# Second half of the out-product and the MLP's first steps from one table of times with the attention

## The chip, the cores and the metric

The kernel runs on one core of a Trainium2 chip, in one launch. The metric is the time on the device in microseconds. Before the change it is 1292.5 us in the median of three runs (1292.22 to 1293.47). The engines are named as in the profile: PE (TensorE), DVE (VectorE), ACT (ScalarE), POOL (GpSimd), SP (SyncE, which here only issues DMAs).

## What is computed

One layer of an encoder on 1024 tokens of 1024 features, in float32:

```
h  = rms(x) * norm1_g
p  = h @ w_in
a  = mlstm_group(conv + silu of p's q and k, v, o, gates)     # 4 heads of 128, both directions
b  = diff_attention_group(q, k, v of p, relative bias)        # 4 heads, softmax - lam * softmax
x  = x + concat(a, b) @ w_out
u  = (rms(x) * norm2_g) @ w_ff1
x  = x + relu(u)**2 @ w_ff2
```

## The kernel before

**Products.** A float32 product is made on PE in three passes of the shorter type fp32r (`mm3`): each operand is cut into a high half (a copy on ACT, `hi`) and a low half (the difference, on DVE or POOL, `lo`); the passes are hi·hi, hi·lo and lo·hi, so that the third matmul of a tile is the first to need the low half of the weights. A matmul has 512 columns here, the transposes and `pav` 128.

**Stages.** From 0 to about 370 us of the span: the projections of x and the mLSTM in small pieces. From 374 to 605: the attention, 32 items (half of the sequence, head, block of 128 queries), with the first half of the out-product (tokens 0 to 511) in between. Then the second half of the out-product (tokens 512 to 1023), and from 660.8 the MLP, up to the end.

**Order.** Inside an engine, instructions run in the order in which the program issues them, and a waiting instruction holds all behind it. Two ways set the order. In the attention a table `A` of times (in items) and `when(t, f, ...)` put small pieces on a heap, and they are issued by ascending time. The mLSTM uses the same heap with its own times, and the MLP a list of its own. The other way is code written out by hand: the second half of the out-product is the generator `out_product(1, psum1)`, whose steps alternate with `row_norms`, `normed`, `cut` and `load_e`, the entry of the MLP:

```
    for n, _ in enumerate(work):
        if n == 2:
            next(norms, None)
        if 3 <= n < 7:
            j = n - 3
            normed(0, j)
            cut(*x_part(1 + j // 2, block(j // 2, 0), j % 2))
        if 6 <= n < 10:
            with tc.issue_after(rooted[0]):
                cut(w_a(n - 6), raw_e[n - 6])
            if n < 8:
                load_e(n - 4)
```

**The out-product's second half.** It has eight tiles n of 128 features; each takes 24 matmuls of 512 columns (8 blocks k in the order 4, 5, 6, 0, 1, 2, 3, 7, three passes each) into the bank `pw1n`. Its weights come as `raw_wo1n` (512 KB, two buffers), `hi_wo1n` and `lo_wo1n` (three buffers each). DVE adds x into `y1` (the row is called `y`), ACT squares it, and DVE sums the squares in `yacc`. `row_norms` makes the row sums on PE (`pr`), adds EPS on DVE, takes the power -0.5 on POOL (`rc`) and spreads the result over the partitions on PE (`pb`). `normed` multiplies y by it, and `cut` makes the halves of the MLP's operands: x1, x2 and later x3 to x7 from y, `wa0`, `wa1`, `wb`, `we` from the loads `re0` to `re3` of w_ff1.

**The attention.** For an item, `pl` are the logits, `l` the weights, `pa` their transposes on PE, `at` DVE's copy of them, `pav` the product with v, `sm` the factors of the rows, `on` the normalised result (DVE). After four items of a head `pt` turns them on PE, and ACT and DVE write the halves into `mix`. In the mLSTM, `pzTrue` are transposes of the stabiliser's rows and `zzTrue` their scaled copies; `pad`, the taps of q and k and `qs` are DVE's, `lo_va` is POOL's low half of the weights of the attention's v.

**In the MLP** `m` are the products, `sq` differences of them, `ro` the odd loads of w_ff1, `z` the products with w_ff2.

Of the kernel before, what the change touches and what calls it, by code (L numbers as in the profile page):

```python
# [10 lines left out]
F32 = mybir.dt.float32  # L11
# [5 lines left out]
P = 128  # L17
# [31 lines left out]
def hybrid_block_kernel(ctx: ExitStack, tc: tile.TileContext, xT, w_v, w_kg, w_c, w_va, w_qa, w_o, w_1, w_2, vec, rel, onehot, outT):  # L49
# [38 lines left out]
    def rsqrt(out, x, n):  # L88
        return nc.gpsimd.tensor_tensor(out, x, mhalf[:, 0:n], op=ALU.pow)
# [67 lines left out]
    def mm3(out, ahi, alo, bhi, blo, start, stop):  # L157
        nc.tensor.matmul(out, ahi, bhi, start=start, stop=False)  # L158
        nc.tensor.matmul(out, ahi, blo, start=False, stop=False)  # L159
        latest[0] = nc.tensor.matmul(out, alo, bhi, start=False, stop=stop).ins  # L160
# [114 lines left out]
            step()  # L275


    clock, table, made = [0.0], [], []

    def when(t, f, *args):  # L280
        heapq.heappush(table, (t, len(made), f, args))
        made.append(t)

    def tick():
# [742 lines left out]
    r2, acc, rooted = {}, {}, {}

    def out_product(half, psum):
        sl = slice(half * HB, (half + 1) * HB)  # L1030
        acc[half] = opool.tile([P, HB], F32, tag="yacc", name=f"yacc{half}")
        order = (4, 5, 6, 0, 1, 2, 3, 7)
        ps, ws = {}, {}

        def load(n):
            if n < KT:
                ws[n] = split(opool, w_o[n], "wo", opool, 3, 2, nc.vector, f"wo{half}{n}")

        def part(n, first, end):
            if first == 0:  # L1040
                load(n)
                ps[n] = psum(n)
            (whi, wlo), p = ws[n], ps[n]
            for j in range(first, end):
                k = order[j]
                kt = slice(k * P, (k + 1) * P)
                mm3(p, whi[:, kt], wlo[:, kt], mix[half][k][:, 0], mix[half][k][:, 1], j == 0, j == KT - 1)


        part(0, 0, KT - 1)  # L1050
        part(1, 0, KT // 2)
        yield
        part(1, KT // 2, KT - 1)
        for n in range(KT):
            if n < 2:
                part(n, KT - 1, KT)
            else:
                part(n, 0, KT // 2)
                yield
                part(n, KT // 2, KT)  # L1060
            p = ps[n]
            yt = y[half][n]
            nc.sync.dma_start(yt, xT[n][:, sl])
            nc.vector.tensor_tensor(yt, p, yt, op=ALU.add)
            if n == 0:
                nc.scalar.activation(acc[half], yt, AF.Square)
            else:
                sq = opool.tile([P, HB], F32, tag="ysq", name=f"ysq{half}{n}", bufs=1)
                nc.scalar.activation(sq, yt, AF.Square)
                nc.vector.tensor_tensor(acc[half], acc[half], sq, op=ALU.add)  # L1070
            nc.scalar.dma_start(y_dram[half][n], yt)
            yield

    def row_norms(half):
        pc = psF.tile([P, HB], F32, tag="q2", name=f"pr2{half}")
        for t in range(4):
            nc.tensor.matmul(pc[:, t : t + 1], acc[half][:, t * P : (t + 1) * P], ones[:, 0:1], start=True, stop=True)
        rc = mpool2.tile([P, 4], F32, tag="rc", name=f"rc2{half}")
        nc.vector.tensor_scalar(rc, pc[:, 0:4], D * EPS, None, op0=ALU.add)
        rooted[half] = rsqrt(rc, rc, 4).ins  # L1080
        yield
        p = psF.tile([P, HB], F32, tag="q3", name=f"pb2{half}")
        for t in range(4):
            nc.tensor.matmul(p[:, t * P : (t + 1) * P], rc[:, t : t + 1].to_broadcast([P, P]), ident, start=True, stop=True)
        r2[half] = mpool2.tile([P, HB], F32, tag=("v", "w")[half], name=f"r2{half}")
        nc.vector.tensor_copy(r2[half], p)
# [93 lines left out]
    def w_out(n):  # L1180
        raw = opool.tile([P, 1024], F32, tag="raw", name=f"raw_wo0{n}", bufs=2)
        hi = opool.tile([P, 1024], F32R, tag="woh", name=f"hi_wo0{n}", bufs=3)
        return hi, opool.tile([P, 1024], F32R, tag="wol", name=f"lo_wo0{n}", bufs=3), raw
# [40 lines left out]
    def item_pieces(n, it):  # L1224
        def on(name, f, *args):
            when(n + A[name], f, it, *args)

        if n % 4 == 0:
            when(n + A["LD"] if n else -98.0, att_load, it)
            when(n + A["LV"] if n else -97.0, att_load_v, it)  # L1230
        for m in range(2):
            on(f"G{m}", att_logits, m)
            on(f"E{m}", att_exp, m)
            on(f"A{m}", att_across, m)
            on(f"C{m}", att_copy, m)
# [16 lines left out]
    last = {}
    while table:
        t, _, f, args = heapq.heappop(table)
        f(*args)
    order.close()
    load_mix(1)
# [6 lines left out]
    work = out_product(1, psum1)
    next(work)
    att_turn(items[28:32], last)
    att_hi(items[31], last)
    att_lo(items[31], last)
# [73 lines left out]
    next(norms)
    for n, _ in enumerate(work):
        if n == 2:
            next(norms, None)
        if 3 <= n < 7:
            j = n - 3
            normed(0, j)
            cut(*x_part(1 + j // 2, block(j // 2, 0), j % 2))
        if 6 <= n < 10:  # L1350
            with tc.issue_after(rooted[0]):
                cut(w_a(n - 6), raw_e[n - 6])
            if n < 8:
                load_e(n - 4)
# [510 lines left out]
```

## Time and profile before

| | us |
|---|---|
| median of three runs | 1292.5 |
| the profiled execution | 1292.14 |
| its span | 1290.4 |
| PE busy | 1257.0 |
| DVE busy | 860.0 |
| ACT busy | 603.5 |
| POOL busy | 272.6 |

The span reaches from the first to the last instruction of the profiled execution, and 1.7 us of its time lie around it. Rows give times from the span's start. An engine's busy time is the sum over its instructions; where PE is nearly always busy, the reader looks for the few stretches in which it stands still and for what ended each of them.

### The profile page before, as it was taken

The numbers are of one execution on the slowest core, as the hardware profiler recorded it, in microseconds if no ns is written. First come the engines' busy times: TensorE is split into PE (matmuls) and PEld (weight loads), VectorE is DVE, ScalarE is ACT, GpSimd is POOL, SyncE is SP. The second block draws the span as 40 slices with busy tenths as digits, with TensorE's granted clock in tenths as the row PEclk, the third lists the DMA queues.
The fourth block names the chain that finished last, engine by engine and source line by source line (L and its number), as shares of the span: only waits on it lengthen the run. The fifth ranks groups of instructions, "written<-read, shape, count | busy, mean of one in ns | idle before, by whom it ended". The sixth has DMA issues, their size and how long they took to land.

```text
span 1290.4 us, 17143 instructions
## 1 busy us (share of the span) xinstructions
PE 1257.0 (97%) x6443; PEld 1038.3 (80%) x6443; DVE 860.0 (67%) x1159; ACT 603.5 (47%) x1033; POOL 272.6 (21%) x273
## 2 busy tenths in 40 slices
PE   8999999999999989999999999999999999999998
PEld 6898678887878877888777788888887888888887
DVE  8635547886338888786748887666664675458754
ACT  5323336676535565563526554454444343333332
POOL 6623312554234344332000000000000000004001
PEclk9999999999999999999989999999999999999999
DMA  6415054544165475526524574454439946344732
GB/s 201 135 54 175 24 190 108 123 123 147 72 201 195 146 263 189 177 98 214 179 95 158 188 244 163 148 163 131 154 118 330 328 163 212 116 145 148 236 114 90
DMA packets 101459, 208.32 MB, mean 161 GB/s; under 512 B 8688, under 2 KB 21744, under 8 KB 101376
## 3 DMA queue, kind: packets, MB, share of 16 engines
q1 hardware_dynamic: 78368, 154.50, 37.6%
q10 hardware_dynamic: 15008, 31.50, 6.5%
q0 software_dynamic: 8000, 21.24, 5.0%
q8 instruction: 50, 0.82, 0.3%
q14 instruction: 33, 0.27, 0.1%
HBM read 148.90 MB, written 58.29 MB: 161 GB/s over the span
## 4 chain that ended last, share of the span: by engine, by line
PE 83%; DVE 8%; DMA 3%; issue 2%; ACT 2%; POOL 1%; SPq 0%; DVEq 0%; ACTq 0%; POOLq 0%
PE z L1707 8%; PE z L1705 8%; PE z L1706 8%; PE m L1376 7%; PE m L1377 7%; PE m L1378 7%; PE pav L986 4%; PE pl L945 3%; PE pv L235 3%; PE pw L158 2%; PE pa L972 2%; PE pw L160 2%; PE pw L159 2%; PE pj_c L158 2%; PE pj_c L159 2%
## 5 line engine op out<-in xcount | busy, mean ns | idle before, releaser
L1743 POOL TENSOR_TENSOR zx<-zx,res 128x512 f32<-128x512 f32 x4 | 8.7, 2180 | 503.8 <-DVE zx L1741 503.8
L1707 PE MATMUL z<-wbh,wa0l 128*128 128x512 f32 x224 | 87.4, 390 | 0.6 <-DVE wa0l L1296 0.6
L1705 PE MATMUL z<-wbh,wa0h 128*128 128x512 f32 x224 | 87.2, 389 | 0.0
L1706 PE MATMUL z<-wbl,wa0h 128*128 128x512 f32 x224 | 87.2, 389 | 0.0
L1706 PE MATMUL z<-wel,wa1h 128*128 128x512 f32 x224 | 87.1, 389 | 0.0
L1705 PE MATMUL z<-weh,wa1h 128*128 128x512 f32 x224 | 87.1, 389 | 0.0
L1707 PE MATMUL z<-weh,wa1l 128*128 128x512 f32 x224 | 87.1, 389 | 0.0
L950 DVE CUSTOM_DVE_ANT_0 l<-pl,toe 128x1024 f32<-128x1024 f32 x64 | 76.3, 1221 | 15.5 <-PE pl L945 14.4
L956 ACT ACTIVATE l<-l,sm 128x1024 f32<-128x1024 f32 x64 | 72.9, 1141 | 1.3 <-DVE sm L950 1.3
L1296 DVE TENSOR_TENSOR wel<-g,weh 128x1024 fp32r<-128x1024 f32 x28 | 35.2, 1258 | 56.5 <-ACT weh L1293 56.5
L1425 ACT ACTIVATE sq<-sq 128x512 f32<-128x512 f32 x48 | 30.3, 632 | 90.6 <-DVE sq L1464 69.0
L1296 DVE TENSOR_TENSOR wbl<-g,wbh 128x1024 fp32r<-128x1024 f32 x28 | 35.4, 1265 | 55.9 <-ACT wbh L1293 55.9
L1293 ACT ACTIVATE weh<-g 128x1024 fp32r<-128x1024 f32 x28 | 29.7, 1060 | 90.2 <-PE z L1707 53.4
L1293 ACT ACTIVATE wbh<-g 128x1024 fp32r<-128x1024 f32 x28 | 29.7, 1061 | 89.9 <-PE z L1707 52.6
L986 PEld LDWEIGHTS pav<-v,at 128*128 128x128 f32 x512 | 62.9, 195 | 9.3 <-DVE on L1001 4.6
L986 PE MATMUL pav<-v,at 128*128 128x128 f32 x512 | 64.4, 280 | 4.5 <-DVE on L1001 2.9
L160 PE MATMUL pw<-mix,lo_wo 128*128 128x512 f32 x128 | 51.5, 402 | 4.2 <-DVE lo_wo L134 4.2
L158 PE MATMUL pj_c<-hhi,hi_c 128*128 128x512 f32 x128 | 53.5, 418 | 0.0
L945 PE MATMUL pl<-kk,q 64*128 64x512 f32 x384 | 53.3, 408 | 0.0
L158 PE MATMUL pw<-mix,hi_wo 128*128 128x512 f32 x128 | 53.2, 415 | 0.0
L159 PE MATMUL pw<-mix,hi_wo 128*128 128x512 f32 x128 | 51.1, 399 | 0.0
L159 PE MATMUL pj_c<-hlo,hi_c 128*128 128x512 f32 x128 | 50.7, 396 | 0.0
(459 smaller groups left out, 3680.2 us busy)
## 6 DMA issues: line engine op xcount, KB each, us to landing
g<-g_dram SPq DMA_DIRECT2D x56, 512.0 KB, 4.1
g_dram<-gs SPq DMA_DIRECT2D x64, 256.0 KB, 4.3
g_dram<-sq ACTq DMA_DIRECT2D x42, 256.0 KB, 2.2
kk<-k_dram POOLq DMA_DIRECT2D x16, 512.0 KB, 5.6
raw_wo<-in_w_o_dram SPq DMA_DIRECT2D x16, 512.0 KB, 4.7
re<-in_w_dram SPq DMA_DIRECT2D x16, 512.0 KB, 4.4
ro<-in_w_dram SPq DMA_DIRECT2D x16, 512.0 KB, 3.7
zt<-in_w_dram SPq DMA_DIRECT2D x16, 512.0 KB, 4.1
```

What stands on the lines that cost most here:

```text
L158: nc.tensor.matmul(out, ahi, bhi, start=start, stop=False)
L159: nc.tensor.matmul(out, ahi, blo, start=False, stop=False)
L160: latest[0] = nc.tensor.matmul(out, alo, bhi, start=False, stop=stop).ins
L945: nc.tensor.matmul(it.pl[x][:, sl], hd.q[r, i, qi * P : (qi + 1) * P], hd.kk[r, j, sl], start=n == 0, stop=n == 2)
L950: nc.vector.tensor_tensor_reduce(lt, it.pl[m], hd.toe[:, off : off + S], 1.0, 3.0e38, ALU.add, ALU.min, it.sm[:, m : m + 1])
L986: nc.tensor.matmul(it.pav[:, 0:P], at, it.head.v[:, c], start=c == 0, stop=c == NC - 1)
L1376: nc.tensor.matmul(p, wh, xh, start=go, stop=False, skip_group_check=True)
L1377: nc.tensor.matmul(p, wh, xl, start=False, stop=False, skip_group_check=True)
L1378: nc.tensor.matmul(p, wl, xh, start=False, stop=stop and k == 3, skip_group_check=True)
L1705: nc.tensor.matmul(p, wh, gh, start=go, stop=False, skip_group_check=True)
L1706: nc.tensor.matmul(p, wh, gl, start=False, stop=False, skip_group_check=True)
L1707: nc.tensor.matmul(p, wl, gh, start=False, stop=end, skip_group_check=True)
```

## The change

The generator `out_product` goes. Its steps become pieces of the table `A`, so that the second half of the out-product and the MLP's first steps are sorted in with the last items of the attention, on every engine: loads with their space (`h_room`, `split_ahead` with a floor in time), matmuls (`h_part`), the sum with x (`h_add`), squares (`h_square`), their sum (`h_sum`), the two steps of `row_norms`, `normed`, and the cuts of x1, x2 and of the first four tiles of w_ff1, high half and low half apart. Besides, 42 pieces of the heap of the attention and the mLSTM and 24 of the MLP's list get an offset to their own time (`moved`), and one entry of `A`, the low half of `mix`, is 0.026 later.

```diff
+    moved = {
+        20: 0.16, 25: -2.784, 36: 2.075, 37: 0.745, 43: -0.133, 92: 2.944, 95: 2.082, 122: -0.259, 124: 2.027,
...
     def when(t, f, *args):
-        heapq.heappush(table, (t, len(made), f, args))
+        heapq.heappush(table, (t + moved.get(len(made), 0.0), len(made), f, args))
...
-        OA=1.385, OW=-3.888, OH=-2.551, OL=-2.267,
+        OA=1.385, OW=-3.888, OH=-2.551, OL=-2.267, HF=34.3, HS=0.375, LM=33, HE=0.3, HQ=0.415, HA=0.425, HW=-1.4,
+        HH=-0.861, HL=-0.4, HX=-3.083, S2=35.3, N0=36.2, N1=36.9, XN=37.278, XD=0.78, XH=1.108, XL=1.118, WN=37.523,
...
-        floor = A["SW"] + 0.01 if pre == "O" else -99.0
+        floor = max(floor, A["SW"] + 0.01 if pre in "OH" else -99.0)
...
-        if n % 4 == 3 and n < 31:
+        if n % 4 == 3:
...
+    def h_part(V, n, first, end):
+        if first == 0:
+            V[0] = psum1(n)
+        k_order = (4, 5, 6, 0, 1, 2, 3, 7)
+        hi, lo, _ = V["w"][0]
+        for j in range(first, end):
+            k = k_order[j]
+            kt = slice(k * P, (k + 1) * P)
+            mm3(V[0], hi[:, kt], lo[:, kt], mix[1][k][:, 0], mix[1][k][:, 1], j == 0, j == KT - 1)
+
+    def h_room(n):
+        nc.sync.dma_start(y[1][n], xT[n][:, HB:])
+
+    def h_add(V, n):
+        nc.vector.tensor_tensor(y[1][n], V[0], y[1][n], op=ALU.add)
...
+    def h_sum(V, n):
+        if n > 0:
+            nc.vector.tensor_tensor(acc[1], acc[1], V["sq"], op=ALU.add)
...
+    parts_at = {0: ((0, 0, 7), (3.5, 7, 8)), 1: ((1.75, 0, 4), (2.75, 4, 7), (3.75, 7, 8))}
+    ends = {0: 3.75, 1: 4.0}
+    for n in range(2, KT):
+        parts_at[n] = ((2 * n, 0, 4), (2 * n + 1, 4, 8))
+        ends[n] = 2 * n + 2.0
+    def room_at(n):
+        return A["HF"] + u * ends[n - 3] + 0.01 if n > 2 else -99.0
+
+    for n in range(KT):
+        t = A["HF"] + u * parts_at[n][0][0]
+        V = {"w": split_ahead(lambda n=n: w_out(n, 1), w_o[n], nc.vector, t, "H", room_at(n))}
+        for p, first, end in parts_at[n]:
+            when(A["HF"] + u * p, h_part, V, n, first, end)
+        t = A["HF"] + u * ends[n]
+        when(max(t + A["HX"], A["S2"] + 0.02), h_room, n)
+        when(t + A["HE"], h_add, V, n)
+        when(t + A["HQ"], h_square, V, n)
+        when(t + A["HA"], h_sum, V, n)
...
+    when(A["N0"], next, norms)
+    when(A["N1"], next, norms, None)
+    for j in range(4):
+        t = A["XN"] + j * A["XD"]
+        when(t, normed, 0, j)
+        when(t + A["XH"], lambda a: cut_hi(*a), x_part(1 + j // 2, block(j // 2, 0), j % 2))
+        when(t + A["XL"], lambda a: cut_lo(*a), x_part(1 + j // 2, block(j // 2, 0), j % 2))
+        t = A["WN"] + j * A["WD"]
+        when(A["RE"] if j < 2 else t - 2 * A["WD"] + A["WL"] + 0.01, load_e, j)
+        when(t, lambda c: cut_hi(w_a(c), raw_e[c]), j)
+        when(t + A["WL"], lambda c: cut_lo(w_a(c), raw_e[c]), j)
...
     def when(t, f, *args):
-        table.append((t, len(table), f, args))
+        table.append((t + moved.get(len(table), 0.0), len(table), f, args))
```

DVE, in the out-product's second half, before: `y0` and `x2` belong to the MLP's entry, `lo_wo16` and `lo_wo17` are the low halves of the weights of tiles 6 and 7.

```order
L1064 TENSOR_TENSOR y1_1_5787<-pw13_5897,y1_1_5787 128x512
L1296 TENSOR_TENSOR x1l_5791<-y0_1_4383,x1h_5790 128x1024
L1070 TENSOR_TENSOR yacc1_5721<-yacc1_5721,ysq13_5928 128x512
L1328 SCALAR_TENSOR_TENSOR y0_2_4384<-y0_2_4384,cst_185,r20_5889 128x512 x2
L1328 SCALAR_TENSOR_TENSOR y0_3_4385<-y0_3_4385,cst_185,r20_5889 128x512 x2
L1296 TENSOR_TENSOR x2l_5793<-y0_2_4384,x2h_5792 128x1024
L1064 TENSOR_TENSOR y1_2_5788<-pw14_5942,y1_2_5788 128x512
L1296 TENSOR_TENSOR x2l_5793<-y0_3_4385,x2h_5792 128x1024
L1070 TENSOR_TENSOR yacc1_5721<-yacc1_5721,ysq14_5973 128x512
L134 TENSOR_TENSOR lo_wo16_6030<-raw_wo16_6028,hi_wo16_6029 128x1024
L134 TENSOR_TENSOR lo_wo17_6069<-raw_wo17_6067,hi_wo17_6068 128x1024
L1064 TENSOR_TENSOR y1_2_5788<-pw15_5991,y1_2_5788 128x512
```

DVE at the same place after the change.

```order
L1233 TENSOR_TENSOR y1_1_5790<-pw13_5893,y1_1_5790 128x512
L1077 TENSOR_TENSOR lo_wo15_5908<-raw_wo15_5906,hi_wo15_5907 128x1024
L1244 TENSOR_TENSOR yacc1_5863<-yacc1_5863,ysq13_5971 128x512
L1305 TENSOR_TENSOR wa0l_5798<-re0_5828,wa0h_5797 128x1024
L1337 SCALAR_TENSOR_TENSOR y0_1_4383<-y0_1_4383,cst_185,r20_5917 128x512 x2
L1337 SCALAR_TENSOR_TENSOR y0_2_4384<-y0_2_4384,cst_185,r20_5917 128x512 x2
L1233 TENSOR_TENSOR y1_2_5791<-pw14_5939,y1_2_5791 128x512
L1305 TENSOR_TENSOR x1l_5794<-y0_0_4382,x1h_5793 128x1024
L1077 TENSOR_TENSOR lo_wo16_5954<-raw_wo16_5952,hi_wo16_5953 128x1024
L1244 TENSOR_TENSOR yacc1_5863<-yacc1_5863,ysq14_6017 128x512
L1305 TENSOR_TENSOR wa1l_5800<-re1_5830,wa1h_5799 128x1024
L1233 TENSOR_TENSOR y1_2_5791<-pw15_5979,y1_2_5791 128x512
```

`lo_wo16` now stands ahead of the sum with the fourth tile's squares and of both cuts of x2, and `lo_wo15` behind tile 3; cuts of w_ff1 (`wa0l`, `wa1l`), which stood further ahead, come between.

SP's queue of DMA issues at the start of the second half, before: `raw_wo1n` are the out-product's weights, `re` w_ff1, `y1` the pieces of x.

```order
L131 DMA raw_wo12_5847<-in_w_o_dram 128x1024
L131 DMA raw_wo13_5891<-in_w_o_dram 128x1024
L131 DMA raw_wo14_5936<-in_w_o_dram 128x1024
L1312 DMA re0_5806<-in_w_1_dram 128x1024
L1312 DMA re1_5808<-in_w_1_dram 128x1024
L1063 DMA y1_0_5786<-in_xT_dram 128x512 x2
L1063 DMA y1_1_5787<-in_xT_dram 128x512 x2
L1063 DMA y1_2_5788<-in_xT_dram 128x512
L131 DMA raw_wo15_5985<-in_w_o_dram 128x1024
```

The same queue after the change.

```order
L1070 DMA raw_wo12_5737<-in_w_o_dram 128x1024
L1230 DMA y1_0_5789<-in_xT_dram 128x512 x2
L1230 DMA y1_1_5790<-in_xT_dram 128x512 x2
L1230 DMA y1_2_5791<-in_xT_dram 128x512
L1321 DMA re0_5828<-in_w_1_dram 128x1024
L1321 DMA re1_5830<-in_w_1_dram 128x1024
L1070 DMA raw_wo13_5838<-in_w_o_dram 128x1024
L1230 DMA y1_2_5791<-in_xT_dram 128x512
L1070 DMA raw_wo14_5857<-in_w_o_dram 128x1024
```

The loads of tiles 3 and 4 went behind five loads of x and two of w_ff1.

DVE in the mLSTM, about 190 us into the span, before: `q0` are taps of the convolution of q, `k4` of k, `pad` is the padded row that they read.

```order
L342 SCALAR_TENSOR_TENSOR zzTrue12_1742<-pzTrue12_1737,cst_185,zzTrue12_1742 128x512
L650 SCALAR_TENSOR_TENSOR q0_1689<-pad_1677,vecs_183,q0_1689 128x1024
L342 SCALAR_TENSOR_TENSOR zzTrue13_1764<-pzTrue13_1759,cst_185,zzTrue13_1764 128x512
L650 SCALAR_TENSOR_TENSOR q0_1689<-pad_1677,vecs_183,q0_1689 128x1024
L646 TENSOR_TENSOR pad_1677<-pj_c4_1682,rb_212 128x1024
L650 SCALAR_TENSOR_TENSOR k4_1788<-pad_1677,vecs_183,k4_1788 128x1024 x4
```

DVE at the same place after the change.

```order
L350 SCALAR_TENSOR_TENSOR zzTrue12_1742<-pzTrue12_1737,cst_185,zzTrue12_1742 128x512
L658 SCALAR_TENSOR_TENSOR q0_1695<-pad_1677,vecs_183,q0_1695 128x1024 x2
L350 SCALAR_TENSOR_TENSOR zzTrue13_1777<-pzTrue13_1772,cst_185,zzTrue13_1777 128x512
L654 TENSOR_TENSOR pad_1677<-pj_c4_1682,rb_212 128x1024
L658 SCALAR_TENSOR_TENSOR k4_1788<-pad_1677,vecs_183,k4_1788 128x1024 x4
```

The piece of `zzTrue13` goes behind the last tap of q and directly ahead of `pad` of the next row; on PE its transposes `pzTrue13` go 12 matmuls back.

## Rows read from the trace of the kernel before

**Rows 1.** The page: busy time of each engine, and the chain that ended last

```profile
PE 1257.0 (97%) x6443; PEld 1038.3 (80%) x6443; DVE 860.0 (67%) x1159; ACT 603.5 (47%) x1033; POOL 272.6 (21%) x273
PE 83%; DVE 8%; DMA 3%; issue 2%; ACT 2%; POOL 1%; SPq 0%; DVEq 0%; ACTq 0%; POOLq 0%
```

**Rows 2.** PE's waits: line waited for, us in total, times, longest us

```profile
PE pw L160 <- DVE lo_wo L134: 4.2, 1, 4.2
...
PE pva L159 <- POOL lo_va L603: 2.6, 2, 1.6
PE m L1376 <- DVE sq L1464: 2.4, 1, 2.4
...
PE m L1377 <- DVE x7l L1296: 0.8, 2, 0.5
```

**Rows 3.** PE in time: start, us, line, op, out<-in, count [idle before <-releaser]

```profile
625.49 1.16 PE L1084 MATMUL pb<-ident,rc 128*128 128x128 f32 x8 [1.43 <-POOL rc L89]
...
643.06 0.39 PE L159 MATMUL pw<-mix,hi_wo 128*128 128x512 f32 x1
647.63 0.80 PE L160 MATMUL pw<-mix,lo_wo 128*128 128x512 f32 x1 [4.18 <-DVE lo_wo L134]
...
652.49 0.63 PE L159 MATMUL pw<-mix,hi_wo 128*128 128x512 f32 x1
```

**Rows 4.** Stretches: us, busy by engine (count), granted PE clock, DMA share, GB/s

```profile
420.00:480.00 60.00, 55.80 (x386) 46.95 (x388) 50.18 (x89) 33.42 (x72) 23.72 (x45) 0.97 0.61 195
600.00:610.00 10.00, 9.99 (x65) 8.66 (x64) 4.26 (x7) 2.92 (x7) 2.06 (x7) 1.00 0.82 289
640.00:650.00 10.00, 5.82 (x22) 4.42 (x21) 9.31 (x12) 4.18 (x5) 0.00 (x0) 0.82 0.09 32
650.00:660.00 10.00, 10.00 (x39) 8.14 (x38) 2.08 (x3) 0.66 (x2) 0.00 (x0) 0.84 0.14 52
```

**Rows 5.** ACT and DVE in time, ahead of the late low half

```profile
637.79 1.04 ACT L133 ACTIVATE hi_wo<-raw_wo 128x1024 fp32r<-128x1024 f32 x1
...
640.17 2.73 DVE L1328 SCALAR_TENSOR_TENSOR y<-y,cst,r 128x512 f32<-128x512 f32 x4
...
646.35 2.36 DVE L134 TENSOR_TENSOR lo_wo<-raw_wo,hi_wo 128x1024 fp32r<-128x1024 f32 x2
```

**Rows 6.** The tile `raw_wo`, 560 to 660 us: its loads

```profile
DMA to landing us min/median/max: 3.5/3.9/6.0
```

**Rows 7.** DVE and PE in time, end of the attention

```profile
578.52 3.17 DVE L134 TENSOR_TENSOR lo_wo<-raw_wo,hi_wo 128x1024 fp32r<-128x1024 f32 x1
...
587.20 0.66 PE L1008 MATMUL pt<-ident,on 128*128 128x128 f32 x4 [0.64 <-DVE on L1001]
```

**Rows 8.** PE and DVE in time, first products of the MLP

```profile
699.10 0.50 PE L1378 MATMUL m<-x5h,wel 128*128 128x512 f32 x1 [0.35 <-DVE wel L1296]
...
710.23 0.68 DVE L1464 TENSOR_TENSOR sq<-w,m 128x512 f32<-128x512 f32 x1
```

**Rows 9.** DVE in time, ahead of the first `z`

```profile
980.39 1.22 DVE L1296 TENSOR_TENSOR wa0l<-za,wa0h 128x1024 fp32r<-128x1024 f32 x1
```

**Rows 10.** ACT, DVE and PE in time, mLSTM

```profile
190.10 0.69 ACT L148 ACTIVATE zzTrue<-pzTrue,cst 128x512 fp32r<-128x512 f32 x1 [1.19 <-PE pzTrue L334]
...
192.87 1.23 DVE L646 TENSOR_TENSOR pad<-pj_c,rb 128x1024 f32<-128x1024 f32 x1
...
204.28 0.66 PE L705 MATMUL pk<-ident,k 128*128 128x128 f32 x4 [0.41 <-ACT k L148]
```

**Rows 11.** DVE, POOL and ACT in time, halves of the attention's v weights

```profile
292.99 1.76 DVE L756 TENSOR_TENSOR qs<-q,qs 128x1024 f32<-128x1024 f32 x1
...
293.62 3.35 POOL L603 TENSOR_TENSOR lo_va<-raw_va,hi_va 128x1024 fp32r<-128x1024 f32 x1
...
297.06 1.04 ACT L148 ACTIVATE hi_va<-raw_va 128x1024 fp32r<-128x1024 f32 x1
```

**Rows 12.** DVE in time, an item of the attention

```profile
467.65 0.35 DVE L1001 TENSOR_SCALAR on<-pav,sm 128x128 f32<-128x128 f32 x1 [0.48 <-POOL sm L89]
```

More of the change, by code (lines that the diff above doesn't have):

```diff
@@ L275, in drain @@
             step()
+    moved = {
[5 rows of a table added]
+    }
     clock, table, made = [0.0], [], []
     def when(t, f, *args):
-        heapq.heappush(table, (t, len(made), f, args))
+        heapq.heappush(table, (t + moved.get(len(made), 0.0), len(made), f, args))
         made.append(t)
@@ L1025, in load_mix @@
             nc.gpsimd.dma_start(mix[half][h], mx_dram[h][half])
[L1027 to L1072, printed above, removed]
+    r2, acc = {}, {}
     def row_norms(half):
@@ L1079, in row_norms @@
         nc.vector.tensor_scalar(rc, pc[:, 0:4], D * EPS, None, op0=ALU.add)
-        rooted[half] = rsqrt(rc, rc, 4).ins
+        rsqrt(rc, rc, 4)
         yield
@@ L1092, in hybrid_block_kernel, with split_ahead @@
         G0=-0.05, G1=0.219, E0=0.984, E1=1.396, W=1.626, A0=2.667, A1=2.819, C0=2.714, C1=2.824, P=3.534, SQ=3.666,
-        RS=3.676, ON=3.783, TU=4.131, TH=4.141, TL=4.151, LD=-2.901, LV=-1.095, PF=-4, PS=1.015, PE=0.388, PT=1.671,
+        RS=3.676, ON=3.783, TU=4.131, TH=4.141, TL=4.177, LD=-2.901, LV=-1.095, PF=-4, PS=1.015, PE=0.388, PT=1.671,
         PB=1.957, PW=-3.566, PH=-2.613, PL=-1.973, PX=-0.258, SW=15.195, OF=18.423, OS=0.979, OE=0.323, OQ=0.587,
-        OA=1.385, OW=-3.888, OH=-2.551, OL=-2.267,
+        OA=1.385, OW=-3.888, OH=-2.551, OL=-2.267, HF=34.3, HS=0.375, LM=33, HE=0.3, HQ=0.415, HA=0.425, HW=-1.4,
+        HH=-0.861, HL=-0.4, HX=-3.083, S2=35.3, N0=36.2, N1=36.9, XN=37.278, XD=0.78, XH=1.108, XL=1.118, WN=37.523,
+        WD=0.8, WL=0.227, RE=35.494,
     )
     clock[0] = -99.0
-    def split_ahead(tiles, src, lo_eng, t, pre):
+    def split_ahead(tiles, src, lo_eng, t, pre, floor=-99.0):
         T = {}
@@ L1178, in hybrid_block_kernel, with w_out @@
     ypool = yq = y = cctx = opool = None
[L1180 to L1183, printed above, removed]
+    def w_out(n, half=0):
+        raw = opool.tile([P, 1024], F32, tag="raw", name=f"raw_wo{half}{n}", bufs=2)
+        hi = opool.tile([P, 1024], F32R, tag="woh", name=f"hi_wo{half}{n}", bufs=3)
+        return hi, opool.tile([P, 1024], F32R, tag="wol", name=f"lo_wo{half}{n}", bufs=3), raw
     def first_half():
@@ L1251, in hybrid_block_kernel, with h_square @@
         item_pieces(n, it)
[L1252 to L1257, printed above, removed]
+    def h_part(V, n, first, end):
[11 more added lines that the diff above has]
+        nc.vector.tensor_tensor(y[1][n], V[0], y[1][n], op=ALU.add)
+    def h_square(V, n):
+        if n == 0:
+            acc[1] = opool.tile([P, HB], F32, tag="yacc1", name="yacc1")
+        V["sq"] = acc[1] if n == 0 else opool.tile([P, HB], F32, tag="ysq", name=f"ysq1{n}", bufs=1)
+        nc.scalar.activation(V["sq"], y[1][n], AF.Square)
+        nc.scalar.dma_start(y_dram[1][n], y[1][n])
+    def h_sum(V, n):
+        if n > 0:
+            nc.vector.tensor_tensor(acc[1], acc[1], V["sq"], op=ALU.add)
     def psum1(n):
@@ L1262, in psum1, with run @@
         return psF.tile([P, HB], F32, tag=f"q{4 + n % 4}", name=f"pw1{n}")
[L1264 to L1268, printed above, removed]
+    when(A["LM"], load_mix, 1)
+    u = A["HS"]
+    parts_at = {0: ((0, 0, 7), (3.5, 7, 8)), 1: ((1.75, 0, 4), (2.75, 4, 7), (3.75, 7, 8))}
[15 more added lines that the diff above has]
+        when(t + A["HA"], h_sum, V, n)
+    def run(until):
+        while table and table[0][0] < until:
+            _, _, f, args = heapq.heappop(table)
+            f(*args)
+    run(A["S2"])
     bctx.close()
@@ L1334, in x_part @@
         return xf[i], src[j], (slice(None), slice(2 * j, 2 * j + 2))
-    load_e(0)
-    load_e(1)
-    next(work)
     psctx.close()
@@ L1341, in hybrid_block_kernel @@
     norms = row_norms(0)
[L1342 to L1354, printed above, removed]
+    when(A["N0"], next, norms)
[9 more added lines that the diff above has]
+        when(t + A["WL"], lambda c: cut_lo(w_a(c), raw_e[c]), j)
+    run(1e9)
+    order.close()
     cctx.close()
@@ L1360, in hybrid_block_kernel @@
     order.enter_context(tc.manual_schedule())
+    moved = {
[3 rows of a table added]
+    }
     table = []
     def when(t, f, *args):
-        table.append((t, len(table), f, args))
+        table.append((t + moved.get(len(table), 0.0), len(table), f, args))
     bank = {}
```

7 rows, old and new, of the table moved are left out of this document.

## Prediction

> **What bounds the kernel now.** I read the page first: TensorE (PE) is busy 97% of the span of 1290.4 us, and it heads the chain that ended last [rows 1]. So the time is PE's work plus the stretches in which PE stands still or runs on the lower clock; another engine matters only where PE waits for it. The view of PE's waits gives those by size [rows 2]; this change touches several of its lines. The reader is to see that the two largest of those in the out-product and the MLP are DVE's: 4.2 us for one half of a split weight tile (`lo_wo`), 2.4 us for one difference (`sq`).
>
> PE's order in time shows what a wait costs. In the out-product's second half, matmuls follow each other every 0.23 us; then one starts at 643.06 and the next at 647.63 [rows 3]. That is 4.57 us between starts, 4.34 lost. The next ones last 0.63 us instead of 0.39, until about 652.9, and the granted clock of the two 10-us stretches is 0.82 and 0.84 [rows 4]: after the idle stretch PE ran at 1.2 GHz instead of 2.4. Thirteen matmuls start 0.43 apart instead of 0.23, another 2.6 us. So this one late tile costs 6.9 us, far more than the 4.2 of the waits.
>
> Why was it late? Its high half is done on ACT at 637.79 + 1.05 = 638.8. DVE makes the low half only at 646.35: from 640.17 on it normalises y and cuts x2 for the MLP [rows 5], which PE reads at 660.8 at the earliest. The order on DVE is at fault, not its load. The small product `pb`, behind a POOL power, costs 1.6 us in the same way (its row says 1.43) [rows 3].
>
> **The change, part by part**, against the profiled execution (1292.14 us; 0.36 below the median of the three runs). I carry the new order along the old clock with the durations of the rows.
>
> *Second half of out_product.* The last attention product `pav73` now comes after seven eighths of the first tile, the tile itself starts at 604.0, and PE meets this work: four groups of 128-column matmuls, 192 matmuls of 512 columns at 0.228, `pr`, `pb`. Followed without a wait, PE starts tile 3 (`pw13`) at 623.7, tile 4 at 630.1, and then one each 5.5 us: 635.6, 641.1, 646.6, and reaches the MLP at 652.1. The third matmul of a tile, 0.47 later, needs the low half. When is it made? Raw loads go into two buffers, so load n+2 is issued when low half n is done; a load lands after 3.9 us (longest 6.0) [rows 6], ACT needs 1.05, DVE 1.22. DVE's new order gives the ends 619.7, 626.7, 632.3, 639.7 and 643.3 for tiles 3 to 7, against 624.2, 630.6, 636.1, 641.6, 647.1 wanted. The least slack is 1.9 us, at tile 6, so the 4.34 and the clock go: -6.9. `pb` comes 12 matmuls into tile 3, at 626.5; `pr` (622.9) plus 0.8, the small DVE operation and 1.56 for the power end at 625.7: -1.6. The bounds for both together are -8.5 (nothing waits) and, if the low half of tile 6 comes 4 us later than I have it, -2 (a new wait of about 2 us and a new stretch of low clock).
>
> What hides the moved work: the five y1 loads (256 KB) and two of w_1 (512 KB) now stand on SP's queue ahead of the load of tile 3. From 604.1 on these and two weight tiles are 3.3 MB; the stretch 600 to 610 moved 289 GB/s [rows 4], so they land by about 615.5, and DVE wants them at 618.4. The load of tile 7 stands behind `re2`, which waits for `wa0l` (634.1): it lands at 639 and is wanted by 645.
>
> *Attention's end.* The split of tile 0 on DVE took 3.17 us [rows 7] instead of 1.22, beside a split of POOL's own; it moves to 602.8, where POOL has only small operations. Then `on72` no longer comes late and PE's 0.64 before `pt` goes [rows 7]: -0.7.
>
> *MLP entry and its 24 moved pieces.* From `pb` of the second half on, PE and DVE start from the same point as before, so only the order counts. PE waits four times there: 0.35 for `wel` [rows 8], twice for `x7l`, 0.8 together, and 2.4 for `sq` [rows 2]; between starts this loses 0.5 + 1.2 + 2.6, and nine matmuls at low clock lose 1.8: 6.1 in all. In the new order `wel` and both `x7l` are ahead of the pieces that stood before them, so the first three go. `sq` comes after `x4l` of the first half, `wd1l` and one difference, without two sums of `ro1`: at 706.6 instead of 710.23 [rows 8]. PE, now 1.7 us earlier at that place, wants it at 706.4 and gets it at 707.4: 1.0 left. But `x4l` of the second half now stands behind three sums of 0.7 and ends at 710.5, where PE wants it at 709.1: 1.4 again, plus 0.6 for two restarts. So 3.0 of 6.1 stay: -3.1. Bounds: -6.1 (both gone) and +1 (a wait of the old size, and the low clock still there).
>
> *Last piece, before the second MLP matrix.* `sq1` goes ahead of `wbl` into idle time of DVE, and `wa0l`, for which PE stands still, starts at 979.8 instead of 980.39 [rows 9]: -0.6 (0 to -0.7).
>
> *mLSTM pieces.* The transposes `pzTrue13` go 12 matmuls back on PE, 2.8 us. Before, ACT copied them at 190.10, and DVE's piece came after that, between two taps of q [rows 10]. Now ACT copies at 192.9 and DVE ends at 194.3; the tap ahead is done at 192.0, so DVE stands still 1.5 us, and `pad`, next in its order, starts at 194.3 instead of 192.87. Taps and silu of k move with it, and PE, which already waited 0.41 for k at 204.28, waits 1.4 more: +1.4 (bounds 0, if a slower tap hides it, and +2.8). PE's two waits for `lo_va` are 2.6 together, the longer 1.6 [rows 2], which leaves 1.0. Of that one: ACT's `hi_va3` goes ahead of the cut of k, which held it until 297.06 [rows 11], when its load had long landed, so POOL can follow at once and the shorter wait goes: -1.0. ACT, held for that landing, is late for k by some 1.8; DVE has 3.1 us idle at 309 to take it up.
>
> The longer one is the question. POOL's `lo_va2` took 3.35 there [rows 11], against 2.36 one tile later. `qs` on DVE ran from 292.99 to 294.75, and 294.75 + 2.36 is 297.1: POOL seems to have begun in earnest only then. `qs` stays ahead, so I leave the 1.6. The Trainium skill (SBUF — State Buffer, section "Who interferes with whom") says the same as a rule: DVE with two SBUF inputs and a POOL instruction that reads SBUF exclude each other, and the later waits for the whole of the other, while one SBUF input does not disturb. `pad`, which reads PSUM and one SBUF tile, then cost POOL nothing, and moving it away gains nothing; if the two shared bandwidth instead, POOL would gain up to 1.0 and the sum would be 1.0 lower. The trace, with 297.1 against an end of 296.97, is on the rule's side.
>
> *Attention pieces.* Five times `on` goes ahead of the copy `at`, twice `pa` ahead of `pav`. PE's product needs both: `on` frees its bank, `at` is its operand. Where `on` waited for POOL (467.65 [rows 12]) the copy, done at 467.2 before, now ends at 468.6, and PE, which started when `on` was done at 468.0, follows: +0.6; elsewhere the two trade places. Part of it is absorbed by DVE's next work; with `pav23` I take +0.5. Bounds: +1.5, and -6.2 if every wait there went (4.4 us, and 1.8 of clock, 0.97 over 60 us [rows 4]). Near the first, since the rows show who ended the wait.
>
> Sum: -6.9 - 1.6 - 0.7 - 3.1 - 0.6 + 1.4 - 1.0 + 0.5 = -12.0. From 1292.14 that is 1280.1, against the median 1280.5.
>
> **Rivals.**
> 1. The MLP entry gives nothing back: `x4l` behind three sums is as late as `sq` was, and the low clock returns. For it: DVE has nearly no idle time from 678 to 711; against it: PE's three small waits surely go. The 3.1 are not gained, and about 1 more is lost: 1284.5.
> 2. The moved attention and mLSTM pieces do take their waits away: -6.2 instead of +0.5, -2.6 instead of +0.4: 1271. For it: every swap stands at a listed wait; against it: the operand stands behind the freed bank.
> 3. The late tile only moves: DVE, some 31 us of work in 38, falls 4 us behind in its new in-order waits (it idles from 619.7 to 624.0 for `pr`), tile 6 is late by 2 us, and the clock falls again: 8.5 shrinks to about 3, 1286.5.
> 4. Slower: SP's queue. Tile 3 was loaded ahead of seven other loads and is now behind them; if y1's space is still held by `pav73`, which now runs to 610.7, 3.3 MB start there. By the rate of 289 GB/s tile 3 lands at about 622, just in time. Beyond that each microsecond costs one, and the clock 2.6; from a landing at about 632 on (half that rate) the gain is gone, at 636 it is 1296. Against it: before, these loads were issued at 604 to 608 without a wait.
>
> **How the numbers follow.** Forecast 0.66 (1278 to 1283 of its own), rival 1 0.17, rival 2 0.06, rival 3 0.07, rival 4 0.04. The forecast and rivals 1 to 3 are all faster by more than 0.2% (2.6 us, about what a measurement can tell here), but 3 in part could end within it: faster 0.92, same 0.04, slower 0.04. The range runs from 1275, between forecast and rival 2, to 1287, past rival 3.
>
> **What would show it.** In PE's waits no `pw` line for `lo_wo` and no `pb` for `rc`; granted clock near 1.0 through the out-product; the MLP's first matmul about 9 us earlier against `pt` of the last head. `m` for `x4l` or `sq` with 1 to 3 us in all. `pk` with about 1.8 instead of 0.41; one `pva` wait instead of two. `pav` for DVE no smaller. It is wrong if a `pw` wait over 1 us or a clock under 0.9 remains in the out-product, or if the waits of the attention are gone.

## The result, and the profile after

The kernel after takes 1275.5 us in the median of four runs (1273.25 to 1276.88), against 1292.4 before: ratio 0.9867, 95% interval 0.985 to 0.9884, 16.9 us faster. Forecast were 12.0 us and 1280.5. The time lies 0.5 inside the lower edge of the range (1275 to 1287) and below the stretch that the forecast gave itself (1278 to 1283). Timed again (e11), the same kernel took 1275.65 against 1292.04.

The profiled execution of after took 1273.25 us, with a span of 1271.4. Its busy times and its chain, as in [rows 1]:

```profile
PE 1248.4 (98%) x6443; PEld 1033.6 (81%) x6443; DVE 855.5 (67%) x1159; ACT 602.3 (47%) x1033; POOL 271.3 (21%) x273
PE 87%; DVE 7%; ACT 2%; issue 2%; POOL 1%; DMA 1%; SPq 0%; DVEq 0%; POOLq 0%; ACTq 0%
```

PE has the same 6443 matmuls; they take 8.6 us less, as matmuls at the lower clock last longer, and the rest is idle time that went. PE's waits of after, which answer to [rows 2]:

```profile
PE pav L994 <- DVE at L985: 3.4, 3, 2.1
...
PE pk L713 <- ACT k L148: 1.7, 1, 1.7
...
PE m L1389 <- DVE x4l L1305: 1.2, 1, 1.2
...
PE pva L159 <- POOL lo_va L611: 0.6, 1, 0.6
```

The lines of `pw` for `lo_wo`, `pb` for `rc`, and `m` for `sq`, `x7l` and `wel` are gone; `pk` for k has grown. The stretches that answer to [rows 4] (here tiles 6 and 7 run from 635.7 to 646.6, and the stretch from 646 to 656 is the first products of the MLP):

```profile
420.00:480.00 60.00, 55.46 (x407) 46.44 (x407) 50.41 (x92) 35.12 (x75) 25.50 (x46) 1.00 0.62 205
600.00:610.00 10.00, 10.00 (x55) 8.56 (x55) 2.96 (x5) 2.97 (x6) 1.01 (x3) 1.00 0.93 313
636.00:646.00 10.00, 10.00 (x46) 8.29 (x45) 9.41 (x11) 3.87 (x5) 0.00 (x0) 1.00 0.63 210
646.00:656.00 10.00, 10.00 (x54) 8.52 (x53) 4.58 (x7) 2.77 (x4) 1.92 (x1) 1.00 0.23 81
```

PE has no idle time left in these tiles, and the granted clock is 1.00 in all four stretches. In order of time, PE's `pb` and the matmul that had waited 4.18 [rows 3], and DVE's low half of tile 6 [rows 5]:

```profile
621.19 1.05 PE L1047 MATMUL pb<-ident,rc 128*128 128x128 f32 x8
...
632.90 1.22 DVE L1077 TENSOR_TENSOR lo_wo<-raw_wo,hi_wo 128x1024 fp32r<-128x1024 f32 x1
...
636.17 0.39 PE L160 MATMUL pw<-mix,lo_wo 128*128 128x512 f32 x1
```

The low half is done at 634.1, 2.0 us before PE wants it; the forecast had 1.9.

Where the time went is read by pairing each matmul with the same one of before and taking the difference of their starts:

| up to (time of before) | after minus before, us | what lies in the step |
|---|---|---|
| 120 | -2.2 | no moved piece; -0.6 by a wait at 9 us, -1.6 by low clock at 22 us, both in before alone |
| 215 | -0.9 | +1.3: `pk` waits for k |
| 310 | -3.3 | -2.6: weights of v (another +0.2 on the way) |
| 474 | -3.0 | +0.35: `at` behind `on` |
| 490 | -4.5 | -1.5: low clock at 476 us in before alone |
| 595 | -5.1 | -0.7: `pt` of the last but one head |
| 660 | -14.2 | -9.1: out-product's second half |
| 720 | -18.8 | -4.6: MLP entry |
| 990 | -19.4 | -0.6: first `z` |

### The profile page after: what moved, and what is told of

It reads as the page before. It is cut to its first block, busy times and chain, and to the rows that moved or that the text cites. A ratio compares the mean times of both kernels' runs of the same rounds, so it can differ in the third digit from the quotient of the medians.

```text
span 1271.4 us, 17135 instructions
## 1 busy us (share of the span) xinstructions
PE 1248.4 (98%) x6443; PEld 1033.6 (81%) x6443; DVE 855.5 (67%) x1159; ACT 602.3 (47%) x1033; POOL 271.3 (21%) x273
## 4 chain that ended last, share of the span: by engine, by line
PE 87%; DVE 7%; ACT 2%; issue 2%; POOL 1%; DMA 1%; SPq 0%; DVEq 0%; POOLq 0%; ACTq 0%
PE z L1719 8%; PE z L1718 8%; PE z L1717 8%; PE m L1389 7%; PE m L1388 7%; PE m L1390 7%; PE pav L994 4%; PE pl L953 3%; PE pv L235 3%; PE pw L158 2%; PE pw L160 2%; PE pw L159 2%; PE pa L980 2%; PE pj_c L158 2%; PE pj_c L159 2%
## 5 line engine op out<-in xcount | busy, mean ns | idle before, releaser
L158 PE MATMUL pw<-mix,hi_wo 128*128 128x512 f32 x128 | 52.3, 408 | 0.0
L160 PE MATMUL pj_c<-hhi,lo_c 128*128 128x512 f32 x128 | 50.5, 395 | 0.0
```

## The experiments

The kernel before was timed beside each of them on the same chip. The runs e1 to e4, e5 to e8 and e9 to e12 are on three different chips, so where a run is set against after, the medians (after took 1275.49 and 1275.65) can be off by what the chips differ, and the larger differences are given by the two ratios to before as well (after 0.9867):

| run | us, median | before, beside it | ratio, 95% interval |
|---|---|---|---|
| e1_tail_only | 1284.17 | 1292.7 | 0.9931 (0.9915 to 0.9946) |
| e2_offsets_only | 1284.21 | 1292.7 | 0.993 (0.9915 to 0.9946) |
| e3_no_mlp_offsets | 1280.73 | 1292.7 | 0.9901 (0.9884 to 0.9917) |
| e4_late_tile6 | 1282.41 | 1292.7 | 0.9919 (0.9906 to 0.9932) |
| e5_no_attention_offsets | 1273.68 | 1291.25 | 0.986 (0.9843 to 0.9876) |
| e6_no_mlstm_offsets | 1279.21 | 1291.25 | 0.9903 (0.9888 to 0.9917) |
| e7_transposes_back | 1274.88 | 1291.25 | 0.9864 (0.985 to 0.9879) |
| e8_x4l_early | 1274.92 | 1291.25 | 0.9869 (0.9855 to 0.9884) |
| e9_hi_va_only | 1288.06 | 1292.04 | 0.9963 (0.9949 to 0.9978) |
| e10_combined | 1275.31 | 1292.04 | 0.9868 (0.9854 to 0.9883) |
| e11_after_again | 1275.65 | 1292.04 | 0.9866 (0.9851 to 0.9882) |
| e12_before_again | 1294.25 (one run) | 1292.04 | |

**The two halves of the change.** The first kernel is after with only the six offsets that belong to the new pieces and the last items, the second is before with all others. In some runs the entries of `moved` are wrapped into other lines; the code cuts show which entries go or come.

```diff
-        20: 0.16, 25: -2.784, 36: 2.075, 37: 0.745, 43: -0.133, 92: 2.944, 95: 2.082, 122: -0.259, 124: 2.027,
...
-        624: -0.106, 629: 0.128, 824: 0.395, 825: 0.395, 826: 0.289, 839: 0.297, 842: -0.289, 944: -0.552,
+        824: 0.395, 825: 0.395, 826: 0.289, 839: 0.297, 842: -0.289, 944: -0.552,
```

> The out-product's second half and the MLP entry in the table of times, without the offsets in the mLSTM, the attention's earlier items and the MLP. Theory (each stage keeps its own share of the 19.0 us between the two profiles): only the 9.3 us of the out-product's end come, so 1292.4 - 9.3 = 1283. In the trace the k transposes wait about 0.4, the two lo_va waits are back (2.6 together), and the MLP's first products wait for wel, x7l and sq as before. Rival (the MLP waits were late leftovers of the out-product, and the offsets there do nothing): 1278 to 1279.

> The kernel before, its hand-written out-product kept, with the offsets of the mLSTM, the attention and the MLP. Theory: the MLP entry gives 4.7, the first z 0.9, the weights of v about 2.0 less 1.2 for the k transposes, the attention between +0.6 and -1.1: 1292.4 - 6 = 1286, with the 4.2 us wait for lo_wo and the low clock behind it still there. Rival (offsets give the larger share): under 1283.

8.5 us each by the medians, 17.0 together: the halves add up, and the offsets, which the forecast had at -2.8 (with the first z and the MLP), bring as much as the out-product.

**The MLP's offsets.**

```diff
-        15: 0.182, 117: 0.641, 118: 0.463, 119: 0.14, 125: 0.086, 139: -0.54, 403: 0.444, 404: 0.722, 405: 0.623,
...
-        663: 0.859, 668: 0.021, 677: 0.348, 682: 1.979, 690: 0.26, 1087: -0.076,
```

> The kernel after without the 24 offsets of the MLP. Theory: the MLP's waits of before come back, with the stretch of low clock behind sq, and the wait of the first z: 4.7 + 0.9 = 5.6 slower than after, 1281. Rival (the earlier start of the MLP entry carries the gain): within 1 us of after.

5.1 to 5.2 us slower than after by the medians, 4.4 by the ratios: the theory in the time. The `sq` wait is back, yet this time without the low clock that the theory had behind it; the waits for `x7l` and `wel` are longer than in before (1.3 and 1.1 in all against 0.8 and 0.4). PE's waits:

```profile
PE m L1384 <- DVE sq L1472: 2.4, 1, 2.4
PE m L1385 <- DVE x7l L1305: 1.3, 2, 1.0
...
PE m L1386 <- DVE wel L1305: 1.1, 2, 0.8
```

The stretch around that wait, with its clock ahead of the DMA share:

```profile
698.00:708.00 10.00, 7.35 (x30) 5.40 (x31) 9.31 (x13) 7.25 (x11) 0.00 (x0) 1.00 0.21 79
```

So the same wait of 2.4 us has low clock behind it in before and none here.

**The price of a late tile.**

```diff
-            lo_eng.tensor_tensor(l[:, 0:1024], raw[:, 0:1024], h[:, 0:1024].bitcast(F32), op=ALU.subtract)
+            for _ in range(times):
+                lo_eng.tensor_tensor(l[:, 0:1024], raw[:, 0:1024], h[:, 0:1024].bitcast(F32), op=ALU.subtract)
...
-        V = {"w": split_ahead(lambda n=n: w_out(n, 1), w_o[n], nc.vector, t, "H", room_at(n))}
+        V = {"w": split_ahead(lambda n=n: w_out(n, 1), w_o[n], nc.vector, t, "H", room_at(n), 6 if n == 6 else 1)}
```

> The kernel after, with the low half of tile 6's weights written six times instead of once (the same values, five more DVE instructions of 1.22 us), so that it is ready about 4 us later than PE wants it: 6.1 - 2.1 of slack. Theory: PE waits 4.0 and then runs at 1.2 GHz for some microseconds, as before the change: 6.5 us slower than after, 1282. Rival (the low clock had another cause): 4.0 slower, 1279.5, clock 1.00 throughout.

6.8 to 6.9 us slower than after by the medians, 6.7 by the ratios; the theory had 6.5. In order of time on PE:

```profile
641.80 0.50 PE L160 MATMUL pw<-mix,lo_wo 128*128 128x512 f32 x1 [2.52 <-DVE lo_wo L1078]
...
657.29 1.02 PE L1040 MATMUL pr<-ones,yacc 128*128 128x1 f32 x8 [2.02 <-DVE yacc L1245]
```

The stretch behind the first of them:

```profile
640.00:650.00 10.00, 8.20 (x29) 6.66 (x30) 9.97 (x13) 2.65 (x3) 0.00 (x0) 0.83 0.30 100
```

The sizes inside are not as expected: seven products of the MLP moved ahead of the late matmul in PE's order and filled part of the wait, so that 2.5 us are lost there and 2.0 more at `pr`, for which they were meant to be the cover. A wait of 1.0 for `sq` follows in the MLP, which after does not have. The low clock (0.83 over 10 us, 1.7 us of work) is there, against the rival. So the run shows that a late tile costs more than its wait; it does not show the price of the wait and the clock alone.

**The attention's offsets.**

```diff
-        191: 0.883, 195: -0.031, 214: 0.154, 226: 0.157, 541: -0.106, 558: 0.172, 563: 0.047, 576: -0.046,
...
-        624: -0.106, 629: 0.128, 824: 0.395, 825: 0.395, 826: 0.289, 839: 0.297, 842: -0.289, 944: -0.552,
+        191: 0.883, 195: -0.031, 214: 0.154, 226: 0.157,
+        824: 0.395, 825: 0.395, 826: 0.289, 839: 0.297, 842: -0.289, 944: -0.552,
```

> The kernel after without the 15 offsets of the attention's earlier items. Theory (the attention's gain is a stretch of low clock that went, not a wait): PE's longest wait there is 1.5 for on again instead of 2.1 for at (0.6 less), and 3.4 us at 1.2 GHz are back near 476 us (1.7 more): 1.1 slower than after, 1276.6. Rival (the forecast: the offsets cost 0.5 and nothing else): 1275.0, clock 1.00 there.

The rival holds and the theory falls. PE's wait is 1.5 for `on` again:

```profile
PE pav L992 <- DVE on L1007: 2.9, 3, 1.5
```

The clock of the stretch that had 0.97 before [rows 4] is 1.00:

```profile
420.00:480.00 60.00, 55.80 (x411) 46.56 (x409) 51.03 (x93) 36.20 (x76) 25.51 (x45) 1.00 0.64 206
```

So the low clock at 476 us was chance: the second profiles of the two kernels bear it out, as before has none near there in e12, and after has it at 468 us in e11. The swaps cost some 0.6 in the trace, near the forecast (0.5); by the ratios it is 0.9 us and by the medians 1.8, within the scatter. In after, DVE at that place, which answers to [rows 12]:

```profile
464.31 0.35 DVE L1009 TENSOR_SCALAR on<-pav,sm 128x128 f32<-128x128 f32 x1 [1.08 <-POOL sm L89]
464.58 0.68 DVE L985 COPY at<-pa 128x512 f32<-128x512 f32 x1
```

`at` stands behind an `on` that waits for POOL, and PE behind `at`.

**The mLSTM's offsets.** After without the 21 entries from 20 to 226 (e6), before with one of them alone (e9), and after with the transposes put back (e7).

```diff
-        20: 0.16, 25: -2.784, 36: 2.075, 37: 0.745, 43: -0.133, 92: 2.944, 95: 2.082, 122: -0.259, 124: 2.027,
...
-        191: 0.883, 195: -0.031, 214: 0.154, 226: 0.157, 541: -0.106, 558: 0.172, 563: 0.047, 576: -0.046,
+        541: -0.106, 558: 0.172, 563: 0.047, 576: -0.046,
```

> The kernel after without the 21 offsets of the mLSTM. Theory (they free the halves of v's weights): the k transposes wait 0.2 to 0.4 instead of 1.7 (1.3 less), but hi_va and lo_va keep PE waiting 2.6 to 3.9 instead of 0.6 (2.0 to 3.3 more): 1276.2 to 1277.5, and up to 1.7 more where the clock falls there. Rival (the forecast: +1.4 for k against -1.0 for lo_va, so without them 0.4 faster): 1275.1.

> The kernel before with a single offset: ACT's high half hi_va3 stands four instructions earlier, ahead of the cut of k. Theory (this one piece is the mLSTM's gain): PE waits 0.6 for lo_va and no longer for hi_va, 2 to 4 us faster than before, some 1289, with the k transposes at 0.2 to 0.4. Rival (the forecast: only the shorter lo_va wait goes): 1.0 faster, 1291.4.

```diff
+    moved = {
+        25: -2.784,
+    }
+
     def when(t, f, *args):
-        heapq.heappush(table, (t, len(made), f, args))
+        heapq.heappush(table, (t + moved.get(len(made), 0.0), len(made), f, args))
```

```diff
-        20: 0.16, 25: -2.784, 36: 2.075, 37: 0.745, 43: -0.133, 92: 2.944, 95: 2.082, 122: -0.259, 124: 2.027,
+        20: 0.16, 25: -2.784, 37: 0.745, 43: -0.133, 92: 2.944, 95: 2.082, 122: -0.259, 124: 2.027,
```

> The kernel after with one offset gone: the transposes pzTrue13 and DVE's piece behind them stand where they stood before. Theory (this move alone costs the 1.3 us that k comes later): 1274.2, k's wait about 0.4. Rival (a later wait takes the time up again): 1275.5.

Without them the kernel is 3.6 to 3.7 us slower than after by the medians and 4.7 by the ratios, and the single offset of `hi_va3` makes before 4.0 us faster by the medians and 4.8 by the ratio (its interval is 2.8 to 6.6), both the theory. PE's waits without the mLSTM's offsets (e6):

```profile
PE pva L159 <- POOL lo_va L609: 2.0, 1, 2.0
PE pva L158 <- ACT hi_va L148: 1.9, 1, 1.9
```

The clock there:

```profile
296.00:306.00 10.00, 6.16 (x26) 4.75 (x25) 9.79 (x12) 3.37 (x4) 2.37 (x1) 0.83 0.32 105
```

PE's wait with the one offset (e9), where that for `hi_va` is gone:

```profile
PE pva L159 <- POOL lo_va L607: 0.6, 1, 0.6
```

The transposes put back (e7) bring k's wait to 0.2, and PE's later matmuls are 1.5 earlier, of which 0.7 is lost again at `lo_va`; by the medians 0.6 to 0.8 faster than after, not clear of noise.

**The last wait of the MLP entry, and a combination.**

```diff
-        663: 0.859, 668: 0.021, 677: 0.348, 682: 1.979, 690: 0.26, 1087: -0.076,
+        663: 0.859, 668: 0.021, 670: -0.185, 677: 0.348, 682: 1.979, 690: 0.26, 1087: -0.076,
```

> The kernel after with one more offset in the MLP: the second low half of x4 stands ahead of the three sums of ro1 on DVE. Theory (PE's 1.2 us wait for x4l is an order on DVE): the wait goes, 1.3 faster than after, 1274.2. Rival (the three sums, 1.2 later, hold PE at wbl or wel instead): 1275.5.

The rival holds: the wait for `x4l` is gone, and five matmuls later PE has a new one of the same size, behind the sums that now come later:

```profile
697.98 0.50 PE L1388 MATMUL m<-x6h,wbh 128*128 128x512 f32 x1 [1.34 <-ACT wbh L1302]
```

> The kernel after without the 15 offsets of the attention's earlier items and without the one that puts the transposes pzTrue13 back. Theory (both cost): 0.6 for the copy at and about 1.0 for k are gained, 1.6 faster than after in the same call. Rival (either is taken up later): no difference from after beyond 0.5.

This is after with the edits of e5 and e7 together. No difference from after (1275.31 against 1275.65). Both waits are smaller, as in e5 and e7, but a new one of 0.74 for `sq` stands in the MLP entry; no version tried is faster than after by more than the intervals of the ratios.

**Both kernels again.**

> The kernel after as it is, for a second profile and for times on the same chip as the others. Theory: 1275.5, the same waits of PE, and low clock at other places than in the first profile, so that a single profile's stretch of low clock outside the long waits is chance.

> The kernel before as it is, for a second profile. Theory: the waits for lo_wo, sq and pb as in the first; low clock behind lo_wo again; around lo_va either 2.6 as in the first profile or 3.9 as in the two kernels without the mLSTM's offsets, by which of POOL and DVE comes first. Rival: 2.6 again, and the 3.9 has another cause.

After shows the same waits, with low clock at 21 and 468 us, where its first profile has none. Before shows another picture around `lo_va`, here PE's waits:

```profile
PE pva L159 <- POOL lo_va L603: 1.9, 1, 1.9
PE pva L158 <- ACT hi_va L148: 1.9, 1, 1.9
```

The clock of that stretch:

```profile
296.00:306.00 10.00, 6.16 (x25) 4.79 (x24) 9.79 (x13) 2.60 (x3) 2.37 (x1) 0.72 0.35 107
```

In the same kernel's first profile PE waited 2.6 there, and the clock was 1.00; here it is low from 300.4 to 307.3 us. Up to 310 us this execution is 3.8 us behind the first one, counted from 280.

## Why the prediction was right, and where its sizes were off

The signs that the forecast named are there: no `pw` line for `lo_wo` and no `pb` line, `pk` at 1.7, one `pva` wait, `m` for `x4l` at 1.2, and `pav` for DVE at 3.4, not smaller. The mechanisms were right; two sizes were not.

**Late tile, `pb` and `pt`: right.** -9.1 against -8.5 for the first two, -0.7 against -0.7, by the pairs; e1 gives -8.5 for all three by the medians and -9.8 by its pairs with before. The low halves came within 0.6 us of the times forecast. e4 shows what a late tile costs, though not apart from what it moves. Rivals 3 and 4 (DVE or SP's queue as a new bound) did not come: DVE idles 3.6 us after the low half of tile 3, and though ACT stands 3.0 us for the load of that tile, the low half is done at 614.9, and PE reads it at 618.9.

**MLP entry: mechanism right, size too small.** -4.6 instead of -3.1. The step that failed is the leftover of `sq`: it was to be 1.0 us late with a restart and is ready in time, and only `x4l` remains, 1.2 instead of 1.4: that is the 1.5 between the two. DVE starts it at 691.57, which is 705.8 in the old clock (14.2 gained ahead of it) and not 706.6. PE and DVE in order of time, as in [rows 8]:

```profile
691.57 0.68 DVE L1476 TENSOR_TENSOR sq<-w,m 128x512 f32<-128x512 f32 x1
692.40 0.47 PE L1388 MATMUL m<-x4h,wd0h 128*128 128x512 f32 x1
...
695.50 0.50 PE L1389 MATMUL m<-x4l,wd0h 128*128 128x512 f32 x1 [1.23 <-DVE x4l L1305]
```

It is ready only just: in e4, e8 and e10 PE waits 1.0, 0.3 and 0.7 for it. e8 shows why the wait for `x4l` does not give way: behind it stands the sum that `wbh` needs.

**First `z`: right**, -0.6; PE no longer waits for it. DVE's piece of [rows 9] is now:

```profile
960.97 1.22 DVE L1305 TENSOR_TENSOR wa0l<-za,wa0h 128x1024 fp32r<-128x1024 f32 x1
```

980.39 less the 18.83 gained ahead of it is 961.56, so it stands 0.6 earlier, as forecast. **Attention: right in size**, +0.35 to +0.6; the 1.5 us that the two profiles show besides is chance (e5, e11, e12). **k: right**, +1.3 against +1.4, on ACT and PE, as in [rows 10]:

```profile
190.51 0.69 ACT L148 ACTIVATE zzTrue<-pzTrue,cst 128x512 fp32r<-128x512 f32 x1 [3.80 <-PE pzTrue L342]
...
203.35 0.66 PE L713 MATMUL pk<-ident,k 128*128 128x128 f32 x4 [1.68 <-ACT k L148]
```

**Weights of v: mis-sized, and the largest miss.** Forecast -1.0, measured -2.6 by the pairs and -4.0 by the medians of e9. The step that failed is "`qs` stays ahead, so I leave the 1.6". That the two instructions hold each other up is borne out; what I took as fixed is who comes first. POOL, DVE and ACT in order of time in the second profile of before (e12):

```profile
287.00 2.39 POOL L603 TENSOR_TENSOR lo_va<-raw_va,hi_va 128x1024 fp32r<-128x1024 f32 x1
287.12 2.30 DVE L797 TENSOR_SCALAR nd<-nd 128x4 f32<-128x4 f32 x1
...
292.87 2.38 POOL L603 TENSOR_TENSOR lo_va<-raw_va,hi_va 128x1024 fp32r<-128x1024 f32 x1
293.32 3.01 DVE L756 TENSOR_TENSOR qs<-q,qs 128x1024 f32<-128x1024 f32 x1
...
297.50 1.24 ACT L148 ACTIVATE k<-pad,vecs 128x1024 f32<-128x1024 f32 x1 [1.86 <-DVE pad L646]
298.65 1.04 ACT L148 ACTIVATE hi_va<-raw_va 128x1024 fp32r<-128x1024 f32 x1
```

The same code gave 3.35 for `lo_va` and 1.76 for `qs` in the first profile [rows 11]. Where POOL starts first, here by 0.1 to 0.5 us, its piece takes 2.4, and DVE's takes 1.8 more than it does elsewhere in these profiles (2.30 against 0.54 for `nd`, 3.01 against 1.21 for the `qs` before it); where DVE starts first, by 0.6, POOL's takes 1.0 more. `nd` has one input, so the forecast's clause that one SBUF input does not disturb is too wide.

The order changes from one execution to the next: POOL is first in 13 of the 14 profiles, in e12 of the kernel before too, and was second only in the one that the forecast had. (In that one the piece two ahead of the first `lo_va` on POOL waits 1.28 us for a DMA, and in e12 it does not; that would explain it, but no run shows it alone.)

With POOL first, `lo_va2` is early, but `qs` ends 1.6 us later, and DVE's `pad` behind it, and with `pad` ACT's first tap of k (the forecast's "cut of k"). `hi_va3`, which stands behind that tap, starts at 298.65 instead of 297.06 and is what PE waits for: 1.9, then 1.9 to 2.0 for the low half made from it, and then the clock, 1.7 us in e6 (0.83 over 10 us) and at least 2.8 in e12 (0.72). That is what the one moved piece takes away: by the pairs e9 gains 2.1 us there on the first profile of before and 5.9 on the second, and the 4.0 of the medians lies between.

The Trainium skill says it on the page that the forecast cites (SBUF — State Buffer, "Who interferes with whom"): the order of issue decides who blocks. The runs agree, by the 2.38 and 3.35 above; I used the half of the rule on what excludes what and not this one. So rival 2 came in its half on the mLSTM: with the +1.4 for k in it, the forecast had +0.4 for these offsets and the rival -2.6, and e6 puts them at -3.6 to -4.7. Its half on the attention did not come.

**In sum:** the forecast of -12.0 and the measured -16.9 differ by 4.9: about 3.0 in the weights of v (by the medians of e9) and 1.5 in the MLP entry (by the pairs); the rest is within the scatter of the medians. By the halves, the out-product was forecast at 9.2 and brings 8.5 (e1), and the offsets were forecast at 2.8 and bring 8.5 (e2). That the time still lies inside the range is in part luck: its lower edge was put between the forecast and rival 2, which had a chance of 0.06, and not at a larger gain of the forecast's own terms. Of the 19.0 us between the two first profiles, 2.2 lie ahead of the first moved piece and 1.5 at 476 us; of these 3.7, all but the first 0.6 are the clock, and none is the change.

## What to carry to other kernels

A wait's cause in one profile can be one side of a race: where instructions of two engines hold each other up and start within some 0.6 us of each other, price the wait for both orders, and look for the piece that is next late in the other one. A late tile on a busy PE costs its wait, and often 1.7 us or twice that through the clock; so pull the piece that PE wants first ahead of those that it wants later, and follow where the pieces behind it end up, since a swap on a full engine only moves the wait.

## What the runs showed of the hardware

Low clock is not set by the length of the wait ahead of it alone. In 10 of 14 profiles the granted clock fell to 1.2 GHz once near 21 us, behind a wait of PE of 2.2 to 3.4 us. In after, e5 and e8 it stayed at 2.4 GHz behind such waits of 2.7 to 2.9, and in e9 behind one of 0.7. Behind the `sq` wait of 2.4 us it fell in before (0.83 over 709 to 719), e1, e9 and e12 and stayed at 1.00 in e3. Two profiles of one kernel can so differ by 2.5 us with the same waits, as the two of after do (1271.4 and 1273.9).

A DVE instruction of 128x4 elements with one input (`nd`) took 2.30 us when it started 0.1 us behind POOL's `lo_va`, and 0.54 when it started 0.5 ahead of it: the size of an instruction does not tell how long it can be held.
